# An FFN's head and tail rearranged: four head tiles slice by slice, the whole tail by token halves, weights in freed tiles

## The chip, the cores and the metric

The kernel runs on one core of a Trainium2 chip. The metric is the device time of one launch in microseconds (us). The kernel before was timed three times: 2056.33, 2068.01 and 2072.43 us, median 2068.01.

The engines of the core are named as in the profile: PE is TensorE's matmul and PEld its weight load, DVE is VectorE, ACT is ScalarE, POOL is GpSimd, SP is SyncE, which issues most of the loads. They run side by side, each in the order in which its instructions were emitted, and wait for each other by semaphores.

## The reference

A decoder trunk of two layers on 512 tokens of width 1024, in float32. Each layer is a half-step SwiGLU FFN, a mixer, and another half-step FFN. The mixer of layer 0 is a short gated convolution, that of layer 1 a sparse attention ("nsa" below). Every sublayer normalises its input with RMSNorm, scales and shifts it with values computed from a conditioning vector, and adds a gated result to x:

```python
def swiglu(h, w_in, w_out):
    g, u = jnp.split(h @ w_in, 2, axis=-1)
    return (jax.nn.silu(g) * u) @ w_out

for i in range(DEPTH):
    ...
    h = adaln(x, norm_g[i, 0], shift[:, 0], scl[:, 0])
    x = x + HALF * gate[:, 0, None, :] * swiglu(h, ffn_w_in[i, 0], ffn_w_out[i, 0])
    h = adaln(x, norm_g[i, 1], shift[:, 1], scl[:, 1])
    y = short_conv_mixer(...) if i % N_MIXERS == 0 else nsa_mixer(...)
    x = x + gate[:, 1, None, :] * y
    h = adaln(x, norm_g[i, 2], shift[:, 2], scl[:, 2])
    x = x + HALF * gate[:, 2, None, :] * swiglu(h, ffn_w_in[i, 1], ffn_w_out[i, 1])
```

`adaln(x, g, shift, scale)` is `rms_norm(x, g) * (1 + scale) + shift`. The FFN's hidden width is 2816 (22 tiles of 128). Attention has 16 heads in 4 groups and three branches (compressed, selected, window).

## The kernel before

**Layout.** x stays in SBUF as 8 tiles of 128 features by 512 tokens. Every product of float32 values is made of three matmuls in a rounded type (`mm3`, L170 to L172): each operand is split into a rounded part hi and a rest lo (`split`, L166 on ScalarE, L167 on VectorE), and hi*hi, hi*lo and lo*hi are summed in PSUM. Weights are loaded as raw float32 tiles of 512 KB by `weights` (L174) and split on the chip; the pool `wp` has three raw, three hi and three lo tiles for them, taken in turn.

**Sublayers.** There are six: the first FFN (`ffn_first`), conv, two FFNs (`ffn`, sublayers 2 and 3), nsa (4) and the last FFN (5). The instructions of each engine stand in an order that a scheduler makes from the program order and from marks of high priority; within an engine they run strictly in that order.

**Between two sublayers.** The next norm needs all 8 tiles of x. So the last part of a sublayer's output, its *tail* (L359), is computed by token halves of 256: first all its output tiles for tokens 0 to 255, then for 256 to 511. After each output tile (`ty`), `residual` adds it to x on VectorE (L326), ScalarE squares it (L223), VectorE sums the squares (`nacc`, L225). When a half is complete, `finish` (L235) takes row sums on TensorE (`pr`, L242), an inverse square root in some twelve small VectorE operations, a diagonal, and a matmul that spreads it over the partitions (`pr`, L250). The next sublayer's *head* (`head_start`, L333) then makes the normalised pieces (`Norm.piece`, L293) and starts on projections that need only the first half, while the second half's chain runs. Of its tiles (`hs`, four in an FFN and in nsa, three in conv) the first three (two in nsa) go slice by slice of k, the others after them; the first half's pieces have high priority, the second half's not.

A piece is `xr` = x times the spread norm (VectorE, L297), `hi` (ScalarE, L299), the full value `hfull` or `hf` (ScalarE or VectorE in turn, L302 and L304), and lo = full - hi (VectorE, L305).

**An FFN** (L460). After the head's two hidden tiles come a third (`pair`, 48 matmuls of 128x512) and then 19 by `seven_products` (L473): a Strassen-like scheme on four blocks of h and of the weights, with 84 matmuls of 128x256 in place of 96. It needs sums of the weights (`qa` by accumulating DMAs, `qb` on VectorE at L490 and L491, their hi and lo) and sums of h: `quarters` (L307) makes t0 to t3 from `hfull` on VectorE (128x1024 each) and splits them into th and tl. The hidden tiles are used in four parts (`FOUR`, 6, 6, 6 and 4 tiles); after each, the output of 8 tiles is added to x. In the last part two output tiles are computed with all 512 tokens at once (`y`), and six in the tail, with weights for pairs of output tiles in a pool of their own (`tw`).

**nsa.** Projections, a compressor and then `attend`: 32 units of work with steps of other work between them, among them the first two quarters of the output projection. Its last two quarters are the tail: four 512 KB weights are loaded and split after attention, when the memory of h is free (`er`, `eh`, `el`).

Of the kernel before, what the change touches and what calls it, by code (L numbers as in the profile page):

```python
# [20 lines left out]
P = 128  # L21
# [30 lines left out]
def decoder_kernel(ctx, tc, xT, cT, ng, adaw, adab, ffi, ffo, cwi, cw, cwo,  # L52
# [121 lines left out]
    def weights(src, nk, ncol, own=None, held=3):  # L174
        def part(name, dt, bufs):
            return (own or wp).tile([P, nk * ncol], dt, name=name, tag=name, padded_shape=[P, KD * P], bufs=bufs)

        hi, lo = part("whi", F32R, held), part("wlo", F32R, held)
        raw = part("wraw", F32, 3 if own is None else 2)
# [30 lines left out]
    class Norm:  # L210
# [69 lines left out]
        def alloc(self, hp):  # L280
            self.full = None
            self.hi = [hp.tile([P, T], F32R, name=f"hhi{d}") for d in range(KD)]
            self.lo = [hp.tile([P, T], F32R, name=f"hlo{d}") for d in range(KD)]
            return self.hi, self.lo


        def alloc_seven(self, tt, tq):
            self.full = tq.tile([P, KD, T], F32, name="hfull")
            self.t = [tq.tile([P, KD // 2, HT], F32, name=f"t{j}") for j in range(4)]
# [3 lines left out]
        def piece(self, d, hf):  # L293
            a, b = HALVES[hf]
            sc, sh = mod(self.s, 0, d), mod(self.s, 1, d)
            xr = tmp("xr", HT, "xr")
            nc.vector.tensor_mul(xr, x[d][:, a:b], self.pr[hf][:, 0:HT])  # L297
            hi = self.hi[d][:, a:b]
            nc.scalar.activation(hi, xr, AF.Identity, scale=sc, bias=sh)  # L299
            hf_ = tmp("hf", HT) if self.full is None else self.full[:, d, a:b]  # L300
            if d % 2:
                nc.scalar.activation(hf_, xr, AF.Identity, scale=sc, bias=sh)  # L302
            else:
                nc.vector.tensor_scalar(hf_, xr, sc, sh, op0=ALU.mult, op1=ALU.add)  # L304
            nc.vector.tensor_tensor(self.lo[d][:, a:b], hf_, hi, ALU.subtract)  # L305

        def quarters(self):  # L307
            n = KD // 2
# [24 lines left out]
    def head_start(nrm, h, jobs, both=3):  # L333
        os = [psum("hs") for _ in jobs]

        def go(n, ks, a, b):
            for k in ks:
                w, wc, kw = jobs[n](k)
                project(os[n][:, a:b], w, wc, h, [(kw, k)], k == 0, k == KD - 1, a, b)

        with tc.high_priority():
            for d in range(KD):
                nrm.piece(d, 0)
        for k in range(KD):
            for n in range(both):
                go(n, [k], 0, HT)
        for n in range(both, len(jobs)):
            go(n, range(KD), 0, HT)
        for d in range(KD):
            nrm.piece(d, 1)  # L350
        for k in range(KD):
            for n in range(both):
                go(n, [k], HT, T)
        for n in range(both, len(jobs)):
            go(n, range(KD), HT, T)
        return os


    def tail(s, nrm, jobs, h, ahead):  # L359
        nxt = ahead() if ahead else None  # L360
        for a, b in HALVES:
            for d, w, wc, ks in jobs:
                o = psum("ty")
                project(o[:, 0:b - a], w, wc, h, ks, True, True, a, b)
                residual(s, d, o, nrm, a, b, True)
# [94 lines left out]
    def ffn(s, f, nrm, nxt, w0, ahead):  # L460
        with ExitStack() as es:
            hp = pool(es, "hp", 1)
            h = nrm.alloc(hp)
            in_es = es.enter_context(ExitStack())
            tt = pool(in_es, "tt", 1)
            swa = pool(in_es, "swa", 1)
# [61 lines left out]
            w = w0 + [ffn_in(f, j, c) for j, c in js[len(w0):]]  # L528
# [6 lines left out]
            sw = pool(in_es, "sw", 1)  # L535
            for j in range(nj):
                hid.activate(os[2 * j], os[2 * j + 1])
            for p, (j0, j1) in enumerate(FOUR):
# [4 lines left out]
                last = p == len(FOUR) - 1  # L543
# [703 lines left out]
```

## Time and profile before

| | |
|---|---|
| runs | 2056.33, 2068.01, 2072.43 us |
| profiled execution | 2060.89 us, its span 2058.8 us |
| mean granted TensorE clock | 0.988 |
| instructions in the span | 32164, of them 12404 matmuls |
| busy: PE, DVE, ACT, POOL | 1980.4, 1505.2, 874.3, 266.9 us |
| first FFN ends, conv begins | about 405 us |
| conv ends, FFN 2 begins | about 589 us |
| FFN 2 ends, FFN 3 begins | about 956 us |
| FFN 3 ends, nsa begins | about 1314 us |
| attention ends | about 1669 us |
| last FFN's head begins | about 1699 us |

The boundaries are the times at which TensorE's first `hs` matmul of a sublayer starts. A group row of the profile reads: line, engine, operation, out<-in with shapes, count, then busy us and the mean ns of one, then the idle time of the engine just before and what ended it. A row of waits reads: who waited at which line, for whom, us in total, times, longest. A row of windows: start and end, length, then busy us and number of instructions of PE, PEld, DVE, ACT and POOL, the granted clock of TensorE, the share of DMA engines busy, and GB/s.

### The profile page before, as it was taken

Reading aid. Unit: us, or ns where it says so; the run is one execution under the profiler, and the core shown is the slowest. Engines: PE = TensorE matmul, PEld = TensorE weight load, DVE = VectorE, ACT = ScalarE, POOL = GpSimd, SP = SyncE. Lnnn points to the kernel's source line nnn. Section 1 sums busy time; section 2 is a strip of 40 time slices with the busy share of each in tenths; the row PEclk is TensorE's granted clock in tenths of the full one; section 3 lists DMA queues with packets and bytes.
Section 4 is the critical chain, followed back from the end, with each engine's and each line's share of the span. In section 5 each row is a group of like instructions: output and inputs, shape, how many; then the busy total and the mean of one; then the engine's idle time right before and its main releaser. Section 6 shows DMA issues by size and latency. Waiting matters only on the chain.

```text
span 2058.8 us, 32164 instructions
## 1 busy us (share of the span) xinstructions
PE 1980.4 (96%) x12404; PEld 1771.8 (86%) x12404; DVE 1505.2 (73%) x2634; ACT 874.3 (42%) x1361; POOL 266.9 (13%) x395
## 2 busy tenths in 40 slices
PE   5999999999999999998999999999999989999999
PEld 3878888888888899998889999898888788898988
DVE  8878888664477677677867677885887878675865
ACT  3322222332244343335534334554777856343432
POOL 0000000100011111110101111001344530111100
PEclk9999999999999999999999999999999999999999
DMA  8888988322234555552545555233111133465642
GB/s 308 301 309 320 330 308 322 126 92 82 92 96 125 144 149 156 149 159 59 154 134 151 156 139 143 100 103 94 52 47 28 41 98 96 134 164 151 164 114 81
DMA packets 110309, 307.37 MB, mean 149 GB/s; under 512 B 14795, under 2 KB 15067, under 8 KB 110156
## 3 DMA queue, kind: packets, MB, share of 16 engines
q1 hardware_dynamic: 88956, 259.86, 36.9%
q0 software_dynamic: 21200, 45.46, 11.3%
q8 instruction: 97, 1.59, 0.3%
q14 instruction: 56, 0.46, 0.1%
HBM read 302.12 MB, written 3.15 MB: 148 GB/s over the span
## 4 chain that ended last, share of the span: by engine, by line
PE 39%; DVE 7%; ACT 3%; issue 2%; SPq 1%; DMA 1%; POOL 0%; ACTq 0%; POOLq 0%; DVEq 0%
PE gu L170 6%; PE gu L171 6%; PE gu L172 6%; PE y L170 4%; PE y L172 4%; PE y L171 4%; DVE L L972 1%; DVE wlo L167 1%; PE nat L170 1%; PE nat L172 1%; PE nat L171 1%; PE s L962 1%; PE ty L172 1%; SPq L881 1%; PE ty L171 1%
## 5 line engine op out<-in xcount | busy, mean ns | idle before, releaser
L166 ACT ACTIVATE whi<-wraw 128x1024 fp32r<-128x1024 f32 (+2 forms) x292 | 291.1, 1000 | 587.8 <-PE y L171 249.7
L167 DVE TENSOR_TENSOR wlo<-wraw,whi 128x1024 fp32r<-128x1024 f32 (+2 forms) x292 | 335.3, 1151 | 66.0 <-ACT whi L166 63.8
L170 PE MATMUL gu<-hhi,whi 128*128 128x256 f32 (+1 forms) x808 | 265.8, 329 | 2.0 <-ACT whi L166 2.0
L171 PE MATMUL gu<-hlo,whi 128*128 128x256 f32 (+1 forms) x808 | 265.6, 329 | 0.0
L172 PE MATMUL gu<-hhi,wlo 128*128 128x256 f32 (+1 forms) x808 | 264.9, 328 | 0.0
L170 PE MATMUL y<-ahi,whi 128*128 128x512 f32 x611 | 241.1, 398 | 3.8 <-ACT ahi L166 3.8
L172 PE MATMUL y<-ahi,wlo 128*128 128x512 f32 x611 | 243.9, 399 | 0.0
L171 PE MATMUL y<-alo,whi 128*128 128x512 f32 x611 | 242.9, 398 | 0.4 <-DVE alo L167 0.4
L121 DVE CUSTOM_DVE_ANT_0 adaraw<-adaraw,cond 128x1024 f32<-128x1024 f32 x144 | 174.5, 1222 | 27.2 <-DMA adaraw<-in_adaw 25.4
L487 POOL DMA_DIRECT2D qa<-in_ffi x114 | 104.3, 1015 | 645.2 <-DMA qa<-in_ffi 542.9
L170 PEld LDWEIGHTS gu<-hhi,whi 128*128 128x128 f32 x808 | 152.1, 188 | 18.2 <-ACT whi L166 3.9
L171 PEld LDWEIGHTS gu<-hlo,whi 128*128 128x128 f32 x808 | 151.8, 188 | 14.4
L172 PEld LDWEIGHTS gu<-hhi,wlo 128*128 128x128 f32 x808 | 152.1, 188 | 14.0
L166 ACT ACTIVATE qbh<-qb 128x1536 fp32r<-128x1536 f32 x57 | 85.0, 1491 | 165.2 <-PE gu L171 143.9
L170 PEld LDWEIGHTS y<-ahi,whi 128*128 128x128 f32 x611 | 114.9, 189 | 36.5 <-ACT ahi L166 8.6
L554 DVE SCALAR_TENSOR_TENSOR x<-y,mods,x 128x512 f32<-128x512 f32 x72 | 54.0, 750 | 120.7 <-PE y L172 120.7
L171 PEld LDWEIGHTS y<-alo,whi 128*128 128x128 f32 x611 | 115.7, 189 | 29.2 <-DVE alo L167 0.8
L172 PEld LDWEIGHTS y<-ahi,wlo 128*128 128x128 f32 x611 | 115.6, 189 | 26.7
L170 PE MATMUL gu<-th,qah 128*128 128x256 f32 x456 | 129.8, 285 | 6.3 <-ACT p L512 6.3
L172 PE MATMUL gu<-th,qal 128*128 128x256 f32 x456 | 129.6, 284 | 0.0
L171 PE MATMUL gu<-tl,qah 128*128 128x256 f32 x456 | 129.5, 284 | 0.0
L172 PE MATMUL gu<-th,qbl 128*128 128x256 f32 x456 | 129.0, 283 | 0.0
(284 smaller groups left out, 5141.2 us busy)
## 6 DMA issues: line engine op xcount, KB each, us to landing
adaraw<-in_adaw SPq DMA_DIRECT2D x144, 512.0 KB, 5.9
wraw<-in_ffi SPq DMA_DIRECT2D x119, 512.0 KB, 4.5
qa<-in_ffi SPq DMA_DIRECT2D x114, 256.0 KB, 4.1
qa<-in_ffi POOLq DMA_DIRECT2D x114, 256.0 KB, 5.3
wraw<-in_ffo SPq DMA_DIRECT2D x72, 384.0 KB, 4.2
qb<-in_ffi POOLq DMA_DIRECT2D x57, 256.0 KB, 3.3
wraw<-in_cwi SPq DMA_DIRECT2D x24, 512.0 KB, 3.3
wraw<-in_ffo SPq DMA_DIRECT2D x20, 512.0 KB, 4.4
```

The lines of the kernel that those rows point to most:

```text
L121: nc.vector.tensor_tensor_reduce(out=raw, in0=raw, in1=cond, scale=1.0, scalar=0.0, op0=ALU.mult, op1=ALU.add, accum_out=m)
L166: nc.scalar.activation(hi, src, AF.Copy)
L167: nc.vector.tensor_tensor(lo, src, hi, ALU.subtract)
L170: nc.tensor.matmul(o, sh, mh, start=first, stop=False)
L171: nc.tensor.matmul(o, sh, ml, start=False, stop=False)
L172: nc.tensor.matmul(o, sl, mh, start=False, stop=last)
L487: nc.gpsimd.dma_start(qa[:, i], quart(1, 0), accum_op=ALU.add)
L554: nc.vector.scalar_tensor_tensor(x[d], o, mod(s, 2, d), x[d], op0=ALU.mult, op1=ALU.add)
L881: nc.sync.dma_start(tb[NR * e:NR * (e + 1), q, :], src)
L962: nc.tensor.matmul(sps[:, off:off + n], Q[q][:, i * P:(i + 1) * P], m[:, 0:n], start=(e == 0), stop=(e == 1))
L972: nc.vector.tensor_tensor_reduce(out=Ls[u][:, LOFF[i]:LOFF[i] + n], in0=sps[:, off:off + n], in1=tb[:, q, T - n:T], scale=1.0, scalar=3e38 ...
```

## The change

1. **Pieces.** xr takes the scale in the same operation; lo is one fused operation from xr, shift and hi. The full value isn't made per piece: in an FFN xr is kept in `hfull`, and `quarters` adds the shift with 8 operations of 128x512 on ScalarE.
2. **Head.** All four tiles go slice by slice in both halves, and both halves' pieces have high priority. conv's head has a fourth tile, the first projection of its second output tile (`nx`). The fourth weight of an FFN's head has a pool of its own (`hw`); t0 to t3 are allocated after it is freed, so that t0 and t1 lie over it. nsa's fourth weight has its second half in `nw`.
3. **FFN tail.** All 8 output tiles of the last part go by halves. The first six take all hidden tiles but the last, then the last one. The weights of the last two pairs go to the tiles that th2/tl2 and th0/tl0 have left, by way of the `qa` buffers. Second-half residuals have high priority, in every tail.
4. **nsa's output.** The four weights of its tail are loaded and split within attention, beside units 25, 26, 28 and 29, into tiles of h that are free by then.
5. **Memory.** The pools for th/tl, for qa/qb and for conv's tail weights lie on the other side of SBUF.

Counts of the whole program: matmuls 12360 to 12456 (128x512 96 fewer, 128x256 192 more), ScalarE's activations 1229 to 1217, VectorE's plain two-operand operations 1413 to 1257, those with a scalar 605 to 731; DMAs unchanged.

```diff
     def piece(self, d, hf):
-            xr = tmp("xr", HT, "xr")
-            nc.vector.tensor_mul(xr, x[d][:, a:b], self.pr[hf][:, 0:HT])
+            xr = tmp("xr", HT, "xr") if self.full is None else self.full[:, d, a:b]
+            nc.vector.scalar_tensor_tensor(xr, x[d][:, a:b], sc, self.pr[hf][:, 0:HT], op0=ALU.mult, op1=ALU.mult)
             hi = self.hi[d][:, a:b]
-            nc.scalar.activation(hi, xr, AF.Identity, scale=sc, bias=sh)
-            hf_ = tmp("hf", HT) if self.full is None else self.full[:, d, a:b]
-            if d % 2:
-                nc.scalar.activation(hf_, xr, AF.Identity, scale=sc, bias=sh)
-            else:
-                nc.vector.tensor_scalar(hf_, xr, sc, sh, op0=ALU.mult, op1=ALU.add)
-            nc.vector.tensor_tensor(self.lo[d][:, a:b], hf_, hi, ALU.subtract)
+            nc.scalar.activation(hi, xr, AF.Identity, bias=sh)
+            nc.vector.scalar_tensor_tensor(self.lo[d][:, a:b], xr, sh, hi, op0=ALU.add, op1=ALU.subtract)
 
         def quarters(self):
+            for d in range(KD):
+                nc.scalar.activation(self.full[:, d], self.full[:, d], AF.Identity, bias=mod(self.s, 1, d))
...
+        for hf, (a, b) in enumerate(HALVES):
+            with tc.high_priority():
+                for d in range(KD):
+                    nrm.piece(d, hf)
+            for k in range(KD):
+                for o, job in zip(os, jobs):
+                    w, wc, kw = job(k)
+                    project(o[:, a:b], w, wc, h, [(kw, k)], k == 0, k == KD - 1, a, b)
         return os
...
             with ExitStack() as tq_es:
-                nrm.alloc_seven(tt, pool(tq_es, "tq", 1))
-                os = head_start(nrm, h, [(lambda k, w=w_: (w, 0, k)) for w_ in w])
+                nrm.alloc_seven(pool(tq_es, "tf", 1))
+                with ExitStack() as hw_es:
+                    hw = pool(hw_es, "hw", 1)
+                    w = w0 + [weights(ffi[f, j, c], KD, P, hw, 1, wp) for j, c in js[len(w0):]]
+                    os = head_start(nrm, h, [(lambda k, w=w_: (w, 0, k)) for w_ in w])
+                nrm.alloc_sums(tt, pool(tq_es, "tq", 1))
                 os += pair(f, nj, h)
                 nrm.quarters()
...
+            ws = []
+            for i, d in enumerate(range(0, KD, 2)):
+                if i < 2:
+                    ws.append(ffn_out(f, d, 2, j0, j1))
+                else:
+                    t = (2, 0)[i - 2]
+                    to = [tt.tile([P, KD // 2, HT], F32R, name=f"t{e}{t}").rearrange("p a b -> p (a b)") for e in "hl"]
+                    raw = swa.tile([P, 2, KD * P // 2], F32, name="qa", bufs=2).rearrange("p a b -> p (a b)")
+                    nc.sync.dma_start(raw.rearrange("p (a n) -> p a n", a=2),
+                                      ffo[f, d:d + 2, :, j0 * P:j1 * P].rearrange("d p c -> p d c"))
+                    split(raw, *to)
...
+            early = [(d, psum("ty")) for d in range(6)]
+            for d, o in early:
+                part(o, d, range(n - 1), 0, HT)
+            for d, o in early:
+                part(o, d, range(n - 1, n), 0, HT)
+                with tc.high_priority():
+                    residual(s, d, o, nxt, 0, HT, True)
+            for d, t in [(d, 0) for d in range(6, KD)] + [(d, HT) for d in range(KD)]:
+                o = psum("ty")
+                part(o, d, range(n), t, t + HT)
+                with tc.high_priority():
+                    residual(s, d, o, nxt, t, t + HT, True)
...
-                    w = w0 + [weights(cwi[c], KD, P) for c in range(len(w0), 3)]
-                    cg, v, b = head_start(nrm, h, [(lambda k, w=w_: (w, 0, k)) for w_ in w])
+                    w = w0 + [weights(cwi[3], KD, P, own)]
+                    *os, nx = head_start(nrm, h, [(lambda k, w=w_: (w, 0, k)) for w_ in w])
...
+            def last_weight(i):
+                to = [hp.tile([P, 2, T], F32R, name=f"e{n}", tag=f"{n}{i}") for n in ("hhi", "hlo")]
+                flat = [t.rearrange("p a b -> p (a b)") for t in to]
+                return weights(nwo[2 + i % 2, i // 2], 2, T, to=flat)
...
+            for i, v in enumerate((25, 26, 28, 29)):
+                needed[v].append(lambda i=i: ew.append(last_weight(i)))
```

More of the change, by code (lines that the diff above doesn't have):

```diff
@@ L1 @@
 import math
-from contextlib import ExitStack
+from contextlib import ExitStack, nullcontext
 import numpy as np
@@ L534, in ffn @@
             nj += 1
[L535 removed]
+            sw_es = es.enter_context(ExitStack())
+            sw = pool(sw_es, "sw", 1)
             for j in range(nj):
```

127 lines of the change are left out of this document (48 added, 79 removed).

## The prediction

> **What bounds the kernel now.** I read the page's first rows, then TensorE's windows, its waits by stage, and the groups of single instructions.
>
> ```profile
> span 2058.8 us, 32164 instructions
> PE 1980.4 (96%) x12404; PEld 1771.8 (86%) x12404; DVE 1505.2 (73%) x2634; ACT 874.3 (42%) x1361; POOL 266.9 (13%) x395
> ```
>
> TensorE is busy for 96% of the span, so no other engine can bound the whole. The page's busy time is modelled, so I measure loss in another way: what a stretch lasts, less its matmuls at the rate of a stretch without gaps. The windows below give rate and stretches (after the length: busy us and instruction counts of PE, PEld, DVE, ACT, POOL; granted clock; DMA share; GB/s).
>
> ```profile
> 698.20:758.50 60.30, 60.30 (x506) 60.27 (x505) 48.76 (x60) 28.16 (x34) 10.78 (x14) 1.00 0.62 157
> 430.00:544.00 114.00, 114.00 (x504) 94.38 (x503) 54.65 (x74) 28.43 (x35) 0.00 (x0) 1.00 0.28 92
> 388.50:428.80 40.30, 37.81 (x286) 36.28 (x285) 28.73 (x87) 20.39 (x36) 1.61 (x1) 0.96 0.16 53
> 570.40:664.40 94.00, 89.05 (x649) 84.45 (x649) 70.17 (x134) 45.24 (x66) 12.95 (x15) 0.96 0.44 115
> 926.30:1027.90 101.60, 93.76 (x674) 86.89 (x673) 81.63 (x154) 52.25 (x78) 9.21 (x11) 0.98 0.40 108
> 1289.70:1345.20 55.50, 52.09 (x374) 48.77 (x372) 43.27 (x108) 33.56 (x62) 1.43 (x1) 0.94 0.20 72
> 1669.30:1770.40 101.10, 93.72 (x697) 88.73 (x698) 81.93 (x156) 53.90 (x81) 10.56 (x13) 0.98 0.39 102
> 1345.20:1669.30 324.10, 300.38 (x2073) 272.02 (x2072) 256.98 (x722) 214.41 (x494) 112.10 (x203) 0.97 0.22 66
> 2032.20:2058.80 26.60, 22.86 (x169) 21.43 (x167) 11.90 (x20) 3.05 (x4) 0.00 (x0) 1.00 0.21 80
> ```
>
> The first row is six of the seven-product tiles: six times 84 = 504 matmuls of 128x256 in 60.3 us, **0.1196 us each**, VectorE busy 48.76 of 60.3. The second is conv's projections: 504 of 128x512 in 114.0, **0.2262 each**. The next five are the places that the change touches. I call them B0 to B4: the tail of one sublayer, the head of the next, and after a head that is an FFN's the pair and the first three seven-product tiles. Matmuls from the code, lost time as length minus matmuls at those rates:
>
> - B0, first FFN to conv: 126 (tail) + 144 (head) narrow ones = 32.3 us of 40.3; lost 8.0.
> - B1, conv to the FFN of sublayer 2: 144 + 192 + 252 narrow, 48 wide (the pair) = 81.2 of 94.0; lost 12.8.
> - B2, FFN to FFN: 144 + 192 + 252 narrow, 24 + 48 wide = 86.6 of 101.6; lost 15.0.
> - B3, FFN to attention: 144 + 192 narrow, 24 wide = 45.6 of 55.5; lost 9.9.
> - B4, attention's output to the last FFN: 192 + 192 + 252 narrow, 48 wide = 86.9 of 101.1; lost 14.2.
>
> Together **59.9 us**: all that the change can win in these stretches. What TensorE waits for there, from the waits of these stretches (B0 first, two rows; B1 one; B2 two; B3 one; B4 two; the last row is ScalarE's, in B2):
>
> ```profile
> PE hs L170 <- ACT hhi L299: 1.4, 2, 1.1
> PE pr L250 <- DVE dg L249: 1.0, 1, 1.0
> ...
> PE gu L170 <- ACT p L512: 2.9, 1, 2.9
> ...
> PE y L170 <- ACT ahi L166: 3.5, 1, 3.5
> PE gu L170 <- ACT p L512: 1.6, 1, 1.6
> ...
> PE hs L170 <- ACT hhi L299: 1.4, 1, 1.4
> ...
> PE ty L170 <- ACT eh L166: 3.0, 1, 3.0
> PE gu L170 <- ACT p L512: 1.8, 1, 1.8
> ...
> ACT whi L166 <- DMA wraw<-in_ffo: 3.6, 1, 3.6
> ```
>
> TensorE's waits here are 16.6 us of the 59.9. The granted clock of the five rows takes 0.04 x 40.3 = 1.6, 0.04 x 94.0 = 3.8, 0.02 x 101.6 = 2.0, 0.06 x 55.5 = 3.3, 0.02 x 101.1 = 2.0, together 12.7. What is left, 30.6 us in all ( 4.0, 6.1, 7.9, 5.2 and 7.4), with the smaller waits, I call short losses: slices that come a little late, and the norm's own small matmuls. Where the clock goes down:
>
> ```profile
> 416.00:420.00 4.00, 2.75 (x10) 2.25 (x11) 3.07 (x10) 2.11 (x4) 0.00 (x0) 0.74 0.05 22
> 645.00:650.00 5.00, 4.42 (x24) 4.42 (x25) 4.53 (x6) 1.90 (x4) 0.57 (x1) 0.66 0.37 98
> 1328.00:1332.00 4.00, 4.00 (x20) 4.00 (x21) 3.55 (x11) 2.82 (x6) 0.00 (x0) 0.50 0.00 0
> 1672.00:1676.00 4.00, 3.31 (x18) 3.10 (x19) 3.57 (x5) 3.08 (x4) 2.15 (x4) 0.75 0.62 177
> ```
>
> After each of these stalls the granted clock is 0.50 to 0.75 for 4 to 5 us, which costs 4 x 0.26 = 1.0, 5 x 0.34 = 1.7, 4 x 0.50 = 2.0 and 4 x 0.25 = 1.0 us. I price the clock after one stall at 1.7.
>
> **The change part by part.** Durations of single instructions (mean in ns after the busy time):
>
> ```profile
> L297 DVE TENSOR_TENSOR xr<-x,pr 128x256 f32<-128x256 f32 x80 | 31.6, 414 | 3.4 <-PE pr L250 3.2
> L305 DVE TENSOR_TENSOR hlo<-hfull,hhi 128x256 fp32r<-128x256 f32 x48 | 19.7, 419 | 2.0 <-ACT hfull L302 1.5
> L326 DVE SCALAR_TENSOR_TENSOR x<-ty,mods,x 128x256 f32<-128x256 f32 x64 | 30.7, 482 | 20.9 <-PE ty L172 20.7
> L524 DVE SCALAR_TENSOR_TENSOR e<-e 128x512 f32<-128x512 f32 x57 | 39.1, 686 | 9.1 <-ACT e L523 9.1
> L167 DVE TENSOR_TENSOR alo<-e,ahi 128x512 fp32r<-128x512 f32 x57 | 39.1, 685 | 7.0 <-ACT ahi L166 7.0
> L278 DVE SCALAR_TENSOR_TENSOR hlo<-xr,mods,hhi 128x512 fp32r<-128x512 f32 x8 | 5.9, 746 | 0.0
> L299 ACT ACTIVATE hhi<-xr,mods 128x256 fp32r<-128x256 f32 x80 | 46.5, 595 | 31.2 <-DVE xr L297 30.9
> L302 ACT ACTIVATE hfull<-xr,mods 128x256 f32<-128x256 f32 x24 | 14.1, 587 | 0.0
> L312 DVE TENSOR_TENSOR t<-hfull 128x1024 f32<-128x1024 f32 x3 | 3.6, 1217 | 0.0
> L523 ACT ACTIVATE e<-e 128x512 f32<-128x512 f32 x57 | 36.0, 631 | 69.0 <-DVE e L522 68.6 <-ACT qbh L166 0.4
> L166 ACT ACTIVATE whi<-wraw 128x1024 fp32r<-128x1024 f32 x204 | 215.0, 1059 | 426.7 <-PE y L171 138.6 <-PE gu L171 94.7 <-issue 63.3
> L167 DVE TENSOR_TENSOR wlo<-wraw,whi 128x1024 fp32r<-128x1024 f32 x204 | 249.6, 1227 | 65.7 <-ACT whi L166 63.6
> L204 DVE TENSOR_TENSOR rs_b<-rs_a,nv 128x2 f32<-128x2 f32 x30 | 4.7, 158 | 0.7
> wraw<-in_ffi SPq DMA_DIRECT2D x119, 512.0 KB, 4.5
> ```
>
> *The pieces.* Before, a piece is xr (0.41), hi on ScalarE (0.60), the full value (0.59 on ScalarE or about 0.42 on VectorE, in turn) and lo (0.42): per half head VectorE 8 x (0.41 + 0.42) + 4 x 0.42 = 8.3 us, ScalarE 7.1. After: two fused operations on VectorE and hi on ScalarE. No row has a 128x256 one with two operands in SBUF and a scalar per partition; L278 has it at 128x512, 0.746, where a plain one has 0.685 (L167), and L326 has 0.482 at 128x256. I take 0.48: 8 x 2 x 0.48 = 7.7, ScalarE 4.8. Bounds 6.7 (as plain ones) and 11.9 (as L278, not halved). TensorE's 96 matmuls of a half take 11.5 us, so the pieces are covered except the first.
>
> The Trainium skill, Vector Engine (DVE) Microarchitecture Reference, section 7, states that such an operation with two SBUF sources that are not bf16 runs at half throughput. L524 has two SBUF sources in f32 at 0.686 and L167's plain subtraction 0.685, so this trace does not agree. By the rule each lo would take about 0.36 more, 2.9 us per first half and some 14 over five heads, and the sum would be -9 in place of -23; the row excludes it.
>
> *The head.* Four tiles go slice by slice through both halves. The work that covers the second half's norm chain (squares, row sums, rsqrt, diagonal, pr, xr, hi) grows from 72 matmuls, 8.6 us, to 96, 11.5 us (in conv's and attention's heads the fourth tile is new to the interleave), and the second half's pieces no longer stand behind other VectorE work. *The quarters* (t0 to t3 and their splits: on VectorE 8 x 1.2 = 9.7) go wholly behind the head, because t0 and t1 lie over the fourth weight; before, about half ran within it. New are 8 shifts on ScalarE in 128x512, 0.63 each as L523 has at that size, 5.0 us. The path from the end of the head to the first tile that seven products need: 8 shifts 5.0, t0 and t2 2.4, split 1.06 + 1.23 = 9.7 us. It is covered by the pair (48 x 0.2262 = 10.9) and two products (24 x 0.1196 = 2.9), 13.7. The slack is 4 us and VectorE's other work there (weights' lo's at 1.23, hidden tiles) takes it: I leave the filling stall at 1.7 in each FFN (2.9, 1.6, 1.8 before).
>
> *The FFN tail.* All eight output tiles go by halves, and 6 of them take their first three hidden tiles (54 matmuls, 6.5 us) before the last hidden tile is needed. That is work in front of the 3.5 us wait at B2, whose origin is the ScalarE row: the last hidden tile's split stood behind a weight split that waited for its DMA. The price is 24 wide matmuls turned into 48 narrow ones in three tails and in conv's head: 4 x (48 x 0.1196 - 24 x 0.2262) = +1.3 us.
>
> *New waits.* In the changed order VectorE has, at B2, a sum of weights (qb, here L490) ahead of the first xr; it needs a load that is issued only after a split in the tail and lands 4.5 us later. Queued behind it are all pieces of the head; TensorE waits for them. Between 0 and 4.5; I take 2. At B3 TensorE has the second half's row sums (pr) ahead of the first half's pr and of the head: the whole of both chains must end before the head begins. From the tail's last matmul that is x 0.48, a square priced as hi 0.60, a sum 0.42, rsqrt in twelve operations of 0.16 (1.9), two halves of the diagonal priced as a sum (0.4 each), xr 0.48 and hi 0.60: 5.3 us, and somewhat more with the small matmuls between them. TensorE had no wait at this place. Bounds 0 (the first half's tiles still feed it) and 7; I take 6, and the clock after it 1.7.
>
> The Trainium skill, TensorE: Matmul & The Clock Gate, Part 1, says that a whole idle window of about 3.4 us halves the clock until a busy window has passed. The row at 1328 agrees with the half but not with the window, since the waits ahead of it are 1.4 us and less. By the rule, the three filling stalls that I leave would cost no clock, and the sum would be 3 x 1.7 better, -28.
>
> *Attention.* Four weight splits of its output move into units 25, 26, 28 and 29: 4 x 1.06 on ScalarE, 4 x 1.23 on VectorE. Both ends: 0 (hidden) and 4 x 2.3 = 9 (all on the path).
>
> ```profile
> 1600.00:1620.00 20.00, 17.51 (x104) 14.29 (x104) 16.82 (x54) 17.65 (x44) 10.25 (x20) 1.00 0.15 42
> ```
>
> ScalarE and VectorE are busy for 17.7 and 16.8 of 20 us, TensorE for 17.5: no engine is full, so I take 2. In exchange the 3.0 us wait for these splits behind attention goes (B4), with its clock.
>
> **The sum by stretch,** as what is left of each loss. Of the short losses I keep all at B0, whose tail and first three weights stay as they are, and elsewhere a quarter to a half, since the pieces (7.7 us) no longer set the pace of a half head (11.5).
> - B0: 8.0 becomes short 4.0: **-4**. The waits of 2.4 and the clock go with the longer cover.
> - B1: 12.8 becomes 5.8 (filling stall 1.7, its clock 1.7, short 2.4): **-7**.
> - B2: 15.0 becomes 7.5 (qb 2, filling 1.7, clock 1.7, short 2.1): **-7.5**.
> - B3: 9.9 becomes 8.9 (new wait 6, clock 1.7, short 1.2): **-1**.
> - B4: 14.2 becomes 7.2 (filling 1.7, clock 1.7, short 3.8): **-7**. The 3.0 us wait goes, and the order of osum, which comes ahead of it, stays.
> - Attention **+2**, matmuls **+1.3**, last tail 0: the drain behind its last matmul is unchanged.
>
> Together -26.5 + 3.3 = **-23 us**: 2060.9 (the profiled execution; its span is 2058.8) to 2037.7. The median of the runs shown is 2068.0, 0.35% above the profiled one; on it the forecast is 2068 - 23 = **2045**. About 1%, 20.7 us, is what a measurement of this kernel can tell from no change.
>
> **The rivals.**
> 1. *New waits take the gain.* The shifts and quarters make VectorE and ScalarE the bound behind each FFN head. For it: VectorE is busy for 27.55 of the 29.8 us of B2's head.
>
> ```profile
> 955.70:985.50 29.80, 27.16 (x203) 24.80 (x203) 27.55 (x65) 19.84 (x33) 0.00 (x0) 1.00 0.16 50
> ```
>
> If t0 and t2 come behind the five seven-product operations that the row's period holds beside them (qb twice at L167's 0.7, its lo at 1.5 times 1.23, qa's lo and one weight's lo 1.23 each: 5.7 us), the slack of 4 turns into a stall of 1.6 + 1.7 more at three FFNs (+10), and the qb wait at its end, 4.5, in two heads (+2.5 at B2, +4.5 at B4) with part of the clock adds +8. That gives -5: **2063**. Against it: half the pieces' ScalarE work is gone from the head.
> 2. *Attention slows* (slower). A split's copy on ScalarE waits for its load with the unit's exponentials queued behind it. Attention runs 37 steps in 324.1 us, 8.8 each. If each of the four costs a whole step and the clock after it, 4 x 10.5 = 42 against the 2 taken: +17, **2085**. It decides from (23 + 2) / 4 = 6.3 us for one split. For it: every engine there waits on another in turn. Against: the DMA share is 0.15 there, and a load lands in 4.5 us, half a step.
> 3. *All stalls go*: no qb wait (-2), B3's wait at 3 without clock (-5), filling stalls gone (-5), splits hidden (-2): -37, **2031**.
>
> **How the numbers follow.** Forecast (-12 to -33) 0.62, two thirds of it over 1%; rival 1 0.20; rival 2 0.10; rival 3 0.08. Faster by over 1%: 0.62 x 0.66 + 0.08 = 0.49. Slower by over 1%: some of rival 2 and what no row shows, 0.10. Within 1%: the rest, 0.41. Range: rival 3's end is left out below, rival 2's above: 2028 to 2068.
>
> **What would show it.** B2: no wait of y on ahi; instead one of VectorE's qb on a DMA. B3: pr waits for diagonals or sums for 3 to 6 us at the tail's end, and then a head of about 23 us without gaps. B4: ty no longer waits for eh. FFN heads: about 23 us for 192 matmuls; gu on p between 0.5 and 3 us. Attention's stretch longer by 0 to 9. The prediction is wrong if heads still show half clock, if gu on p grows above 3, or if attention's stretch grows by over 9.

## The result and the profile after

The changed kernel is a little slower: ratio **1.0030** to the kernel before, 95% interval 1.0016 to 1.0044 (medians of 20 runs each: 2066.88 and 2059.77 us; the three runs known at the prediction had a median of 2068.01). Forecast was 2045, some 23 us faster. The span of the profiled execution is 2065.3 us against 2058.8.

The first rows of the page of the changed kernel:

```profile
span 2065.3 us, 32264 instructions
PE 1975.3 (96%) x12500; PEld 1773.4 (86%) x12500; DVE 1499.4 (73%) x2604; ACT 860.2 (42%) x1349; POOL 264.8 (13%) x393
```

Nothing shows there: TensorE is at 96% as before. In the rows below, `gu` is an FFN's hidden tiles, `y` its outputs, `ph` the compressor's first product, `nat` nsa's projections and `s` the first scores of attention; `p` is the copy of a seven-product tile's first product, `qbh` and `ahi` are rounded parts of a sum of weights and of a hidden tile, `wlo` is the rest of a weight, `nacc` the sum of squares and `dg` the norm's diagonal. The windows of the changed kernel, cut at the same instructions as in the prediction (first `ty`, `hs`, `y`, `nat` or `s` matmul of a stage):

```profile
386.50:564.70 178.20, 177.82 (x931) 152.74 (x930) 95.86 (x166) 55.19 (x77) 6.99 (x4) 1.00 0.27 90
564.70:657.50 92.80, 86.02 (x650) 81.81 (x649) 67.69 (x123) 43.11 (x65) 12.78 (x15) 0.98 0.44 115
918.60:1018.20 99.60, 93.86 (x698) 89.64 (x697) 75.59 (x144) 49.30 (x78) 10.63 (x13) 0.97 0.42 110
1018.20:1056.40 38.20, 35.48 (x147) 28.20 (x146) 21.69 (x27) 9.44 (x12) 3.04 (x4) 0.96 0.43 124
1283.30:1339.30 56.00, 50.60 (x398) 49.54 (x397) 39.79 (x101) 22.46 (x44) 1.94 (x2) 0.94 0.26 82
1339.30:1425.40 86.10, 76.68 (x579) 74.11 (x577) 60.75 (x146) 36.68 (x56) 2.13 (x6) 0.94 0.29 92
1425.40:1671.70 246.30, 227.15 (x1496) 200.08 (x1497) 203.16 (x580) 184.81 (x452) 110.74 (x197) 0.97 0.18 52
1671.70:1774.20 102.50, 92.83 (x698) 88.03 (x697) 73.65 (x140) 48.31 (x77) 10.54 (x13) 0.98 0.39 101
1774.20:1871.10 96.90, 93.90 (x651) 86.69 (x650) 69.25 (x87) 37.19 (x44) 13.91 (x18) 1.00 0.58 147
```

and the windows of the kernel before that the prediction does not show and that are needed beside them:

```profile
388.50:570.40 181.90, 179.41 (x907) 152.86 (x906) 96.40 (x173) 59.63 (x83) 6.71 (x4) 0.99 0.26 87
1027.80:1061.60 33.80, 33.80 (x147) 26.95 (x146) 18.80 (x23) 9.05 (x11) 3.76 (x5) 1.00 0.46 143
1345.00:1422.60 77.60, 72.78 (x580) 70.19 (x578) 59.38 (x147) 33.29 (x47) 2.13 (x6) 1.00 0.35 110
1422.60:1672.30 249.70, 227.81 (x1497) 201.96 (x1497) 199.22 (x579) 183.55 (x452) 109.97 (x197) 0.96 0.18 55
1672.30:1770.30 98.00, 93.61 (x697) 88.61 (x698) 80.41 (x154) 51.67 (x78) 10.56 (x13) 0.98 0.38 98
1770.30:1864.20 93.90, 93.90 (x650) 87.05 (x649) 67.44 (x83) 37.26 (x44) 13.95 (x18) 1.00 0.57 152
```

| stretch | before | after | difference | forecast |
|---|---|---|---|---|
| up to the first tail | 388.5 | 386.5 | -2.0 | 0 |
| B0 and the rest of conv | 181.9 | 178.2 | -3.7 | -4 |
| B1 | 94.0 | 92.8 | -1.2 | -7 |
| B2 | 101.6 | 99.6 | -2.0 | -7.5 |
| the output behind B2 | 33.8 | 38.2 | +4.4 | 0 |
| B3 | 55.5 | 56.0 | +0.5 | -1 |
| nsa's projections and compressor | 77.6 | 86.1 | +8.5 | 0 |
| attention, to the first tail matmul | 249.7 | 246.3 | -3.4 | -1 |
| B4 from its first tail matmul | 98.0 | 102.5 | +4.5 | -4 |
| the output and tiles behind B4 | 93.9 | 96.9 | +3.0 | 0 |

(In the forecast column the 3.0 us wait ahead of the tail of nsa is counted to attention, where this cut puts it. The forecast's +1.3 for matmuls is not spread over the rows. The stretches left out add about -2, and with them the rows make up the span's +6.5. The first row is no part of the change: second executions of both kernels had 385.5 and 386.2.) So one end of the change works and another gives it back: the gain stands in B0 and in the FFN tails. The loss stands mostly *behind* the heads, in places that the prediction did not list, and in nsa's tail. The waits of TensorE in the changed kernel, around B1, behind FFN 3's head, B3, the compressor and B4:

```profile
PE pr L251 <- DVE dg L250: 1.9, 1, 1.9
...
PE y L170 <- ACT ahi L166: 2.7, 1, 2.7
PE gu L170 <- ACT p L501: 2.3, 1, 2.3
PE gu L170 <- ACT qbh L166: 1.4, 1, 1.4
...
PE pr L243 <- DVE nacc L226: 2.4, 1, 2.4
PE pr L251 <- DVE dg L250: 1.9, 1, 1.9
...
PE ph L171 <- DVE wlo L167: 6.9, 2, 5.6
...
PE pr L243 <- DVE nacc L226: 3.8, 1, 3.8
```

The wait of y on ahi that stood in B2's tail before (3.5 us) is gone from there, and one of 2.7 stands behind the seven-product tiles. In the compressor the kernel before has this wait at the same place:

```profile
PE ph L171 <- DVE wlo L167: 1.2, 1, 1.2
```

VectorE's side, as a timeline of the changed kernel at the end of FFN 3's head (start, length, instruction, idle time before it and what ended it):

```profile
961.56 0.48 DVE L303 SCALAR_TENSOR_TENSOR hlo<-hfull,mods,hhi 128x256 fp32r<-128x256 f32 x1 [0.75 <-ACT hhi L302]
969.77 2.36 DVE L167 TENSOR_TENSOR wlo<-wraw,whi 128x1024 fp32r<-128x1024 f32 x2 [7.72 <-ACT whi L166]
972.04 1.22 DVE L312 TENSOR_TENSOR t<-hfull 128x1024 f32<-128x1024 f32 x1
973.18 1.22 DVE L313 TENSOR_TENSOR t<-hfull 128x1024 f32<-128x1024 f32 x1
```

VectorE stands for **7.72 us** while TensorE does the second half of the head, and then has two weight splits and the four sums at once. In the kernel before, its longest wait there was half of that:

```profile
DVE wlo L167 <- ACT whi L166: 3.9, 1, 3.9
```

VectorE in the tail of nsa in the changed kernel, with rows between left out:

```profile
1685.22 0.69 DVE L479 TENSOR_TENSOR qb<-qa,wraw 128x512 f32<-128x512 f32 x1 [4.11 <-DMA qa<-in_ffi]
1685.83 0.42 DVE L226 TENSOR_TENSOR nacc<-nacc,sq 128x256 f32<-128x256 f32 x1
...
1689.68 0.42 DVE L226 TENSOR_TENSOR nacc<-nacc,sq 128x256 f32<-128x256 f32 x1 [0.54 <-ACT sq L224]
```

Here it holds everything behind it for **4.11 us** for a DMA, by the sum of weights (`qb`) for a tile that is not needed before the head is over. Four of the first half's seven sums `nacc` stand behind it, and pr starts at 1690.16, right after the last of them.

**How far an execution repeats.** Both kernels were profiled once more.

> The kernel before, a second profiled execution. It shows how far a stage's length differs between executions of the same program. If stages repeat within 1 us, the differences of 3 to 6 us read so far are the change's; the attention stretch (first s to the tail), 242.6 to 252.1 in the kernels profiled, is expected to differ by several us here too, and the others by less than 1.

> The changed kernel, a second profiled execution, for the same purpose: FFN 3's head to its second output 171.8, FFN 3's tail to nsa's head 104.5, nsa's head to the first s 111.3, nsa's tail to the last head 31.2 and the last head to its second output 168.2 us should repeat within 1 us if they are the program's; if they move by 3 or more, the readings by stage are of one execution only.

Lengths in us; h2, h3 and h5 are from an FFN's head (sublayers 2, 3, 5) to its second output `y`, t3 from FFN 2's third output to FFN 3's head, t4 from FFN 3's third output to nsa's head:

| execution | t3 | h2 | h3 | t4 | nsa head to s | s to tail | tail to head 5 | h5 |
|---|---|---|---|---|---|---|---|---|
| before | 103.4 | 169.2 | 166.0 | 98.3 | 108.6 | 249.7 | 27.2 | 164.8 |
| before, again | 103.5 | 169.1 | 165.6 | 98.3 | 108.6 | 249.5 | 27.7 | 164.8 |
| after | 99.4 | 168.5 | 171.8 | 104.5 | 111.3 | 246.3 | 31.2 | 168.2 |
| after, again | 99.6 | 168.5 | 168.6 | 104.5 | 111.1 | 249.1 | 31.3 | 168.0 |

All repeat within 0.5 us but two of the changed kernel: h3 (171.8 and 168.6) and attention (246.3 and 249.1). So of the +4.4 behind B2 some 3 us are of one execution, and attention is not faster. Two more rows of the first table depend on the execution: B4 and the output behind it take 102.5 and 96.9 us in one execution of the changed kernel, 105.6 and 93.7 in the other, so that only their sum, some 7.5 us over the kernel before, is the program's; and B0 with the rest of conv is 3.7 us shorter in the first pair of executions and 2.2 in the second (180.5 and 178.3).

### The profile page after: what moved, and what is told of

Its sections match the earlier page's. It is cut to its first block, busy times and chain, and to the rows that moved or that the text cites. A ratio compares the mean times of both kernels' runs of the same rounds, so it can differ in the third digit from the quotient of the medians.

```text
span 2065.3 us, 32264 instructions
## 1 busy us (share of the span) xinstructions
PE 1975.3 (96%) x12500; PEld 1773.4 (86%) x12500; DVE 1499.4 (73%) x2604; ACT 860.2 (42%) x1349; POOL 264.8 (13%) x393
## 4 chain that ended last, share of the span: by engine, by line
PE 71%; DVE 13%; DMA 8%; ACT 4%; issue 3%; SPq 0%; POOL 0%; DVEq 0%; ACTq 0%; POOLq 0%
PE gu L170 10%; PE gu L171 10%; PE gu L172 9%; PE y L170 7%; PE y L171 6%; PE y L172 6%; DMA adaraw<-in_adaw 4%; DVE wlo L167 2%; PE hs L170 2%; PE hs L171 2%; PE hs L172 2%; DMA qa<-in_ffi 2%; PE cv L170 2%; PE cv L172 2%; PE cv L171 2%
## 5 line engine op out<-in xcount | busy, mean ns | idle before, releaser
L166 ACT ACTIVATE whi<-wraw 128x1024 fp32r<-128x1024 f32 (+2 forms) x286 | 284.7, 999 | 581.6 <-PE y L171 243.4
L167 DVE TENSOR_TENSOR wlo<-wraw,whi 128x1024 fp32r<-128x1024 f32 (+2 forms) x286 | 328.4, 1151 | 90.0 <-ACT whi L166 88.1
L170 PE MATMUL y<-ahi,whi 128*128 128x512 f32 x587 | 232.9, 398 | 5.7 <-ACT ahi L166 5.7
L171 PE MATMUL y<-alo,whi 128*128 128x512 f32 x587 | 233.0, 397 | 0.4 <-DVE alo L167 0.4
L172 PE MATMUL y<-ahi,wlo 128*128 128x512 f32 x587 | 231.9, 395 | 0.0
L170 PEld LDWEIGHTS y<-ahi,whi 128*128 128x128 f32 x587 | 110.1, 188 | 36.4 <-ACT ahi L166 9.8
L171 PEld LDWEIGHTS y<-alo,whi 128*128 128x128 f32 x587 | 110.6, 188 | 27.1 <-DVE alo L167 1.4
L172 PEld LDWEIGHTS y<-ahi,wlo 128*128 128x128 f32 x587 | 110.6, 188 | 27.0
L170 PE MATMUL gu<-th,qbh 128*128 128x256 f32 x456 | 128.8, 283 | 4.2 <-ACT qbh L166 4.2
```

What stands on the lines that cost most here:

```text
L166: nc.scalar.activation(hi, src, AF.Copy)
L167: nc.vector.tensor_tensor(lo, src, hi, ALU.subtract)
L170: nc.tensor.matmul(o, sh, mh, start=first, stop=False)
L171: nc.tensor.matmul(o, sh, ml, start=False, stop=False)
L172: nc.tensor.matmul(o, sl, mh, start=False, stop=last)
```

## The experiments

**Priority of the residuals.** All four places where `after` marks tail residuals:

```diff
-                with ahead_of(a):
-                    residual(s, d, o, nrm, a, b, True)
+                residual(s, d, o, nrm, a, b, True)
```

> The changed kernel with the high priority of the residuals in all tails taken back (both the FFN tails and the second halves of conv's and nsa's). Theory 1 (the priority puts the second half's row sums ahead of tail matmuls in TensorE's order, so TensorE stands for VectorE's sums): the waits of pr on nacc (6.3 us in three places in the changed kernel) go, the nsa tail from its first ty matmul to the first of the following head shrinks from 31.2 to 27 us, FFN 3's tail to nsa's head shrinks by 1 to 3 us; 5 to 8 us faster than the changed kernel in all. Rival (the priority pays for itself by earlier second halves): the waits reappear as waits of hs on hhi or of pr on dg within the heads, and the total stays within 2 us of the changed kernel.

Ratio 1.0005 (0.9983 to 1.0027), about 5 us below the changed kernel; the two intervals overlap, so this gain is not clear of noise. By the trace the expectation is half right: at B3 pr's wait on nacc (2.4) is gone and t4 falls from 104.5 to 101.0. At B4 the wait is as long as before:

```profile
PE pr L243 <- DVE nacc L226: 3.9, 1, 3.9
```

So there it isn't the priority; the wait of qb on its DMA stands there as in the changed kernel (4.2 us), and nsa's tail to the last head takes 32.4.

**The order of the head's tiles.**

```diff
-            for k in range(KD):
-                for o, job in zip(os, jobs):
-                    ...
+            each = list(zip(os, jobs))
+            for part in (each[:both], each[both:]):     # both: 3 in an FFN, 2 in nsa, 4 in conv
+                for k in range(KD):
+                    for o, job in part:
+                        ...
```

> The changed kernel with the order of head tiles as before: three slice by slice and then the fourth in an FFN, two and then two in nsa; conv keeps four. Theory 2 (tiles interleaved slice by slice finish, and free their weights, all at the end, so VectorE and ScalarE stand in the second half of the head, 7.7 us of VectorE at FFN 3's head, and are behind afterwards): VectorE's idle stretch at the end of the FFN heads falls from 7.7 to about 5, and in nsa the copies t<-hs begin before the head's end; the stretch from nsa's head to the first s matmul, 93.1 us in the changed kernel and 84.5 before, returns to 85 to 87; the stretch from FFN 3's tail to the end of the first y after its first three tiles, 137.8 us changed and 135.5 before, falls by 2 to 4. 8 to 12 us faster in all. Rival (t0 and t1 over the fourth weight are what delays the sums): the FFN stretches stay as they are, only nsa's changes, or nothing does.

Ratio 0.9974 (0.9952 to 0.9996), 11 to 12 us below the changed kernel. VectorE's idle stretch at the end of FFN 3's head, from its waits there, and nsa's compressor:

```profile
DVE wlo L167 <- ACT whi L166: 5.3, 1, 5.3
...
PE ph L171 <- DVE wlo L167: 1.4, 1, 1.4
```

5.3 in place of 7.7 us, as expected; h3 is 165.4 (changed: 171.8 and 168.6), h5 164.7, nsa's head to s 104.1. From nsa's first `nat` to s it is 78.6 us, against 86.1 changed and 77.6 before (the expectation counts this stretch from some 7 us earlier: 93.1 and 84.5). With all four tiles slice by slice every tile ends at the end of the head: the 16 copies `t<-hs` on which the compressor's VectorE work hangs start 1.1 us before the head's end (1338.4 of 1339.5) and 6 us before it in the kernel before (1339.2 of 1345.2). The head itself was 5.8 us shorter (25.2 against 31.0), and TensorE then waited for this VectorE work.

**t0 and t2 in memory of their own.**

```diff
-            self.t = [tq.tile([P, KD // 2, HT], F32, name=f"t{j}") for j in range(4)]
+            self.t = [(tq if j % 2 else ta).tile([P, KD // 2, HT], F32, name=f"t{j}") for j in range(4)]
...
+                ta = pool(tq_es, "ta", 1)
                 with ExitStack() as hw_es:
```

> The changed kernel with t0 and t2 in memory of their own and t1 and t3 over the fourth weight, so that t0 and t2 can be made during the head; nothing else is edited. Theory 3 (the memory under t0 is what makes the sums late): VectorE does t0, t2 and their two splits (4.9 us) in its idle stretch of 7.7 us at the head's end; the waits of gu on p (2.6, 2.3, 2.0) and on qbh (1.4 each) and of y on ahi (2.7, 1.9) shrink to below 1 each; 4 us less in each of the three FFNs, 10 to 13 us faster in all. Theory 2 (the weights that come free at the head's end): the sums come early but the weights' splits still start at the end of the head, and only 1 to 2 us go in each FFN, 3 to 6 in all.

Ratio 0.9967 (0.9950 to 0.9984), 13 us below the changed kernel. The sums now fill the idle time (timeline of VectorE in the same head, and what is left of its wait):

```profile
958.46 1.22 DVE L312 TENSOR_TENSOR t<-hfull 128x1024 f32<-128x1024 f32 x1
961.13 1.23 DVE L313 TENSOR_TENSOR t<-hfull 128x1024 f32<-128x1024 f32 x1 [1.06 <-ACT hfull L307]
962.28 2.44 DVE L167 TENSOR_TENSOR tl<-t,th 128x1024 fp32r<-128x1024 f32 x2
```

```profile
DVE wlo L167 <- ACT whi L166: 2.8, 1, 2.8
```

The idle stretch is 2.8 us, h3 falls to 163.9 and h5 to 164.3, both under the kernel before. Theory 3 holds for these two FFNs; h2 gains only 1.0, because there another wait remains (below). gu still waits on p, 3.4 us in two pieces, so the expected "below 1" did not come.

**The three together.**

> All three edits together. If the three causes are separate the gains add up: 20 us or more below the changed kernel and 14 or more below the kernel before. If they share one cause (VectorE behind after the heads) the gain is little more than the largest of the three alone, and the result is within 8 us of the kernel before.

Ratio 0.9944 (0.9923 to 0.9964): 18 us below the changed kernel, less than the 30 that the three add up to alone (5 of them not clear of noise). In the FFNs order and memory are two remedies for one cause, VectorE behind after the head: h3 is 162.5 here against 165.4 and 163.9, and h5 167.0 against 164.7 and 164.3. That h5 is not shorter goes with the clock: from that head to the first output (73.5 us) the granted clock is 0.95, and 0.98 and 1.00 in the two others, which is an estimated 2 and 4 us.

**The sum of weights that stands ahead of the pieces.**

```diff
+            late = sp.tile([P, 1], F32, name="late", bufs=1)
...
+                if j == nj:
+                    nc.vector.tensor_scalar(late, nrm.lo[KD - 1][:, T - 1:T], 0.0, 1.0, op0=ALU.mult, op1=ALU.add)
+                    nc.vector.scalar_tensor_tensor(qb[:, 1], qa[:, 1], late, raw[:, 0], op0=ALU.mult, op1=ALU.add)
+                else:
+                    nc.vector.tensor_tensor(qb[:, 1], qa[:, 1], raw[:, 0], ALU.add)
```

> The changed kernel with one dependency added: the first sum of weights of an FFN's first seven-product tile (qb, L479) is multiplied by a one that is made from the last piece of the head, so it can't stand ahead of the head's pieces. Theory 4 (this sum, moved by the scheduler into the tail ahead of x, squares and pieces, waits for its DMA and holds VectorE): the two waits of qb on the DMA (2.1 us at conv's end, 4.1 at nsa's end) go, and with them pr's waits at these places (1.9 and 3.8): the nsa tail from the first ty to the head falls from 31.2 to about 27, the stretch from conv's tail to the second FFN's first y by 2; 6 to 9 us faster with the clock. Rival (the priority of the residuals or the nsa tail's own order makes pr wait; its undoing left 3.9 there, so this rival is weak): pr still waits for nacc for 3 us or more.

In the trace it does what was expected: qb waits for no DMA, pr for no nacc in B4, and nsa's tail falls from 31.2 to 26.1, h2 by 2.4. So in B4 the sum of weights is the cause of pr's wait. But the time did not follow: ratio 1.0025 (1.0007 to 1.0043). Other stretches had grown, among them some in which only TensorE's pace counts: from FFN 2's second to its third output 94.2 us stand where 93.5 stood, and from the last FFN's second output to the last matmul 191.5 for 190.4. The question comes back below.

**The weight splits within attention.** The weights of nsa's last two groups loaded and split behind attention, as in the kernel before, the rest as changed.

> The changed kernel with the four weight splits of nsa's output taken back behind attention. If the splits cost nothing within attention, the wait of ty on eh (3.0 us before) comes back at the end and the kernel is 3 to 5 us slower than the changed one. If they cost attention what the prediction's second rival says, the stretch from the first s to the last unit shrinks by more than that and it is faster.

Ratio 1.0007 (0.9987 to 1.0027): not slower than the changed kernel (the intervals overlap), against what was expected of it. The wait of ty on eh came back, and longer:

```profile
PE ty L170 <- ACT eh L166: 4.0, 1, 4.0
```

but pr's wait behind it went: the qb sum stands at the same place of VectorE's order and no longer waits for its DMA; tail to head is 28.0 in place of 31.2. From s to the last head it is 278.2 us, and 277.4 and 280.4 in the two executions of the changed kernel (276.9 and 277.2 before): the splits cost attention nothing that can be seen, and their gain was eaten by the next wait in line. A cost of a few us could not be seen, since attention alone takes from 242.6 to 252.5 us in the kernels profiled here.

**Toward a better kernel.** The edits of the priority, the order, t0 and t2, and the sum of weights together (acde), and the same with an FFN's four tiles slice by slice again (best1):

> Residuals without priority, head tiles in the order of before (conv with four), t0 and t2 clear of the fourth weight, and the sum of weights held behind the pieces. The first three gave a ratio of 0.9944 to the kernel before; if the sum of weights is a cause of its own, 6 to 9 us more: 0.990 to 0.992. If it only fills time in which TensorE waits anyway: 0.994.

> As the last, but an FFN's four head tiles slice by slice as in the changed kernel (nsa's two and two). With t0 and t2 clear of the fourth weight the order of the FFN's tiles should matter little if theory 3 holds: within 3 us of the last. If weights that come free late are what counts (theory 2), 4 us or more slower than the last.

acde 0.9940 (0.9918 to 0.9963), best1 0.9918 (0.9898 to 0.9938). With t0 and t2 free, the slice-by-slice order costs the FFNs nothing (theory 3), and the sum's own gain was again not seen in acde: 0.9944 without it. Both have the longer TensorE stretches of e_qb, so this became the question: the one-column tile `late` takes 4 bytes per partition and moves what is allocated after it in SBUF.

```diff
-            late = sp.tile([P, 1], F32, name="late", bufs=1)
+            late = sp.tile([P, 1], F32, name="late", padded_shape=[P, 16], bufs=1)      # or [P, 64]
```

> The kernel best1 (residuals without priority, nsa's head tiles two and two, t0 and t2 clear of the fourth weight, the sum of weights held behind the pieces) with the one-column tile of that last edit padded from 4 to 64 bytes per partition; every engine's instructions are in the same order, only addresses in SBUF move. In all three kernels with the 4-byte tile the stretches that only TensorE sets are longer: 94.2 in place of 93.5 us for four seven-product tiles and the outputs around them, conv's matmuls 0.230 in place of 0.227 us each. Theory 5 (the place of the operands in SBUF sets this): 64 bytes bring 0.227 and 93.5 back, and the kernel is 8 to 14 us faster than best1, a ratio near 0.986. Rival (the added dependence or its place in VectorE's order does it): unchanged, 0.992.

> The same with the one-column tile padded to 256 bytes per partition, again with the same order on every engine. If the addresses' remainder by 64 bytes is what counts, this equals the kernel padded to 64 bytes (0.227 us, 93.5 us, ratio near 0.986). If a larger remainder counts, only this one has 0.227 and the other keeps 0.230. If the dependence is the cause, both keep 0.230 and the ratio stays at 0.992.

Ratios **0.9851** (0.9832 to 0.9871) and **0.9853** (0.9837 to 0.9869): 14 us below best1 by 60 or 252 bytes, with the same instructions in the same order on every engine but for one pair on VectorE (a fill of 60 ns and a weight's rest, in conv). The stretch from FFN 2's first output to its second, one row each from the windows of best1 and of the two padded kernels, in this order:

```profile
656.20:750.40 94.20, 94.20 (x650) 87.35 (x649) 67.48 (x83) 37.16 (x44) 13.96 (x18) 1.00 0.58 152
```

```profile
654.90:747.90 93.00, 93.00 (x650) 86.15 (x650) 67.38 (x83) 37.20 (x44) 13.99 (x18) 1.00 0.60 153
```

```profile
653.30:746.80 93.50, 93.50 (x650) 86.63 (x649) 67.34 (x82) 37.22 (x44) 13.99 (x18) 1.00 0.58 153
```

VectorE and ScalarE are as busy in each; TensorE is without a gap in all three, and has 650 records in 94.2, 93.0 and 93.5 us. The next stretch, from the second output to the third, in e_qb, which has the 4-byte tile, and in f_attend, which has none and ran on the same chip as best1 and e_qb:

```profile
750.50:844.80 94.30, 94.30 (x651) 87.45 (x650) 67.58 (x83) 37.13 (x44) 13.91 (x18) 1.00 0.58 151
```

```profile
751.40:844.90 93.50, 93.50 (x650) 86.64 (x649) 67.36 (x83) 37.21 (x44) 13.92 (x18) 1.00 0.59 153
```

So the chip is not the cause. An estimate of what the pace is worth: in best1 matmuls of 128x256 start on average 119.6 ns apart, in the padded kernels 117.7 and 118.5 (counting distances of 100 to 140 ns, some 7,500 in each trace), those of 128x512 231.4 ns, and 231.1 and 230.6 (200 to 260 ns, some 3,700). That makes 15 and 11 us, so the pace is about the whole gain. Padded to 64 bytes, this is the fastest kernel of the study, together with the one padded to 256, some 30 us below the kernel before.

## Why the prediction was wrong

- **That the time lies within the range is luck.** 2066.88 is inside the stated range of 2028 to 2068, but the range was counted from 2068.01, the median of three runs, and the 20 runs have 2059.77. As a difference the range is -40 to 0 and the forecast -23; measured was +7.
- **The reading of the bound held.** TensorE stayed at 96% while the time grew, and what the change won and lost lay in its waits and short losses. Wrong was what it does to them. B1 to B4 by the prediction's own method (length less matmuls at 0.1196 and 0.2262 us; named waits from 1 us; the clock by the rows; the rest are its short losses), in us:

| B1 to B4 together | before | forecast | after |
|---|---|---|---|
| waits | 14.2 | 13.1 | 24.5 |
| clock | 11.1 | 6.8 | 10.3 |
| short losses | 26.6 | 9.5 | 15.2 |
| lost in all | 51.9 | 29.4 | 50.0 |

  The short losses did fall, by two thirds of what was forecast. The waits took that gain back: in B1, B2, B3 and B4 they are 5.9, 5.0, 5.4 and 8.2, and 2.9, 5.1, 1.4 and 4.8 before.
- **B0, the FFN tail, the pieces: right, B0 in part.** B0 with conv came to -3.7 for -4, and to -2.2 in the second pair of executions. The FFN tail alone, t3, is 4.0 and 3.9 shorter in the two pairs, and y's wait on ahi gone from the tail. The fused operations were priced at 0.48 each and took:

```profile
L300 DVE SCALAR_TENSOR_TENSOR hfull<-x,mods,pr 128x256 f32<-128x256 f32 x48 | 21.3, 475 | 4.2 <-PE pr L251 4.2
L303 DVE SCALAR_TENSOR_TENSOR hlo<-hfull,mods,hhi 128x256 fp32r<-128x256 f32 x48 | 21.8, 479 | 2.5 <-ACT hhi L302 2.3
```

  L303 has two SBUF sources in f32 and isn't slower for it; the Trainium skill's rule of half throughput (Vector Engine (DVE) Microarchitecture Reference, section 7) does not show here either.
- **"The quarters" failed.** The working let them start at the head's end and gave a slack of 4 us, which was then spent on one line ("VectorE's other work takes it: I leave the filling stall at 1.7"). That VectorE would have *nothing to do* in the second half of the head was not worked out: the weights of the pair could not be split, since with slice-by-slice order all wp buffers come free at the end, nor the sums made, since t0 lay over the fourth weight. 7.7 us of VectorE's time are lost there, against 3.9 before, and come back as work behind the head. The waits of gu on p and on qbh, the filling stall, were 4.0, 3.7 and 3.4 us in FFN 2, FFN 3 and the last FFN, not 1.7 each; in FFN 3 y's wait of 2.7 came on top. c_order and d_t02 each shorten VectorE's wait, to 5.3 and 2.8 us, and with it h3; with t0 and t2 free best1 has the slice-by-slice order and no such wait over 0.5 us. This is the prediction's first rival, which had 0.20: right in its mechanism, but its 2063 is -5 against 2068, and +7 came. The shifts, which the rival also blamed, took 0.71 each and were over some 6 us before the head's end, ahead of a stretch in which ScalarE stood idle for 5.3; they did not hold up the sums here.
- **"New waits" was right in kind and wrong in place.** The qb sum was seen at B2 and priced at 2. There it waited for nothing; it waited 2.1 at B1 and 4.1 at B4, where the sum counted none (rival 1 counted 4.5 at B4). B3's wait was priced at 6: 2.4 + 1.9 + 1.1 = 5.4 measured, and B3 came out at +0.5 for -1.
- **The compressor was not in the sum.** The stretches of the forecast ended with nsa's head, and the largest single loss, 8.5 us, came just behind it, from the same change that made that head 5.8 us shorter (net 2.7 from nsa's head to s: 111.3 for 108.6). c_order shows the cause by undoing it.
- **B4** was off by 8.5: -4 (without the wait ahead of it) was forecast, +4.5 came. 4.0 of the +4.5 lie between the tail's first matmul and the head, where pr's wait of 3.8 stands. The clock is not the difference: it is 0.98 over B4 in the rows of both kernels.
- **Attention** was right in cost, about nothing; its gain, the 3.0 us wait, went into the next wait, pr's 3.8.
- **Of the signs of being wrong, one came.** The heads still show half clock: 0.93 over FFN 3's head and 0.91 over nsa's.

```profile
944.30:969.60 25.30, 25.29 (x198) 25.13 (x198) 14.55 (x47) 12.76 (x25) 0.00 (x0) 0.93 0.00 1
1314.10:1339.30 25.20, 25.16 (x194) 25.11 (x195) 15.30 (x34) 9.59 (x20) 0.00 (x0) 0.91 0.11 32
```

  gu on p stayed at or under 2.6 us, and attention did not grow.
- **A term on neither side: the pace of the matmuls.** Between two FFN outputs, without a gap in TensorE's rows, the kernel before takes 93.9 us and the changed one 93.5. Over all 128x256 matmuls that is an estimated 4 us in the change's favour (119.05 against 118.5 ns from start to start, 7,500 of them), so its waits cost more than the +7 shows. The change moves many tiles in memory; which of them does it was not tried.

## What to carry to other kernels

A reordering that closes the gaps of the busiest engine also moves the moment at which results and buffers come free for the others; ask of each engine not only whether its work is covered, but what it can do in the meantime and what then stands behind it. Follow a stage to the point at which the old and the new order meet again, since here the largest loss came just behind the last stretch that was summed. Where two kernels differ by a per cent and no wait explains it, compare stretches without gaps: here 60 bytes of padding were worth 14 us.

## What the runs showed of the hardware beyond that

With the same order on TensorE, ScalarE and GpSimd, one pair swapped on VectorE and no gap in TensorE's rows, the same 650 recorded matmuls took 94.2, 93.0 or 93.5 us, depending on whether a tile of 4, 64 or 256 bytes per partition was allocated ahead of the others; the ratio to the kernel before went from 0.9918 to 0.9851 and 0.9853. What about the addresses counts, their remainder by 64 bytes or the distance of two operands, was not tried. It fits that the edit of e_qb, which has the 4-byte tile too, brought no time although its waits went: its matmuls of 128x256 and 128x512 start 119.6 and 231.5 ns apart, against 118.5 and 230.6 in the changed kernel, by the estimate above some 12 us. But e_qb was not run with a padded tile, so this is argued and not shown.
